# Bias tables of every second neighbourhood head in the two conditioning tiles, with the conditioning rows kept in DRAM meanwhile

## The chip, the cores and the metric

The kernel runs on one core of one Trainium2 chip. The metric is the device time of one execution in microseconds (us); less is better. A core has five engines, each with an instruction queue of its own that is worked off in order: PE (TensorE, matrix products), DVE (VectorE), ACT (ScalarE), POOL (GpSimd) and SP (SyncE, which here only issues DMA transfers). Work of different engines runs side by side unless a semaphore makes one wait for the other.

## The reference

Two layers of a diffusion backbone over 512 latent tokens and 256 context tokens, model width 1024. Both token streams are shifted, scaled and gated by vectors that come from two conditioning rows (`c` for the latent tokens, `c_ctx` for the context tokens):

```python
silu_c = jax.nn.silu(c)[:, None, :]
silu_cc = jax.nn.silu(c_ctx)[None, None, :]
for l in range(DEPTH):
    sh_a, sc_a, g_a, sh_f, sc_f, g_f = jnp.split(silu_c @ mod_w[l] + mod_b[l], 6, axis=-1)
    csh_a, csc_a, cg_a, csh_f, csc_f, cg_f = jnp.split(silu_cc @ mod_w[l] + mod_b[l], 6, axis=-1)
    a_lat, a_ctx = modulate(h_lat, sh_a, sc_a), modulate(h_ctx, csh_a, csc_a)
    ...
```

Layer 0 has 8 latent-attention heads (MLA) and 8 two-dimensional neighbourhood heads; layer 1 has sliding-window attention (SWA) with 16 heads. Each layer ends in a SwiGLU. In a neighbourhood head every query sees a patch of keys, and a learned table by relative place is added to the scores:

```python
s_lat = jnp.einsum('bnqhd,bknmhd->bhnqkm', qr, k_blk).astype(jnp.float32) * scale
s_lat = s_lat + col_bias[:, dr_idx].transpose(0, 2, 3, 1, 4)[None]
s_lat = jnp.where(col_ok[:, :, None, :], s_lat, NEG_INF).reshape(b, h, n_cb, NA_CB, kr * NA_KB)
s_ctx = jnp.einsum('bnqhd,bchd->bhnqc', qr, kc).astype(jnp.float32) * scale
p = jax.nn.softmax(jnp.concatenate([s_ctx, s_lat], axis=-1), axis=-1).astype(v.dtype)
```

## The kernel before

The program is one pass in stages, told here by the profiled execution: the start with norm, first modulation and the values of the neighbourhood heads (0 to 75 us), the input projections with modulation vectors beside them (75 to 195), the neighbourhood heads (195 to about 275), the MLA heads (to about 390), output projection and SwiGLU of layer 0 (to about 1030), SWA (about 1040 to 1180), output projection and SwiGLU of layer 1.

**Order.** The program is written as Python generators and then put in order by a scheduler that plays the program through on a timeline of its own and writes each engine's queue. A changed dependence can therefore move instructions on every engine, also far from the edit. Afterwards each queue is fixed.

**Tiles.** `T(tag, shape)` takes the next buffer of a ring of that name; `BUFS` says how many buffers a ring has, `SIZES` how many bytes each has in a partition. Writing into a buffer waits until all readers of its former tile are done. The ring `nb` has two buffers.

**Conditioning rows.** The tile `cond` holds both rows, each spread over all 128 partitions (2 x 1024 numbers). `load_cond(v)` loads row v by a DMA and applies Silu on ACT. Before that, the same tile serves for a moment as scratch for the shift terms of the values (`raw`). The rows are read by `mod_tile`: a row of `mod_w` is multiplied by the conditioning row and summed, on DVE (L237, and L215 for the late ones), or on POOL and ACT (L254, L255) for the second row during the projections. In the neighbourhood and MLA heads no modulation vector is computed; the next reader is L215 in layer 0's SwiGLU.

**Bias tables.** `nb_tiles(h)` loads the tables of head h as two tiles of the ring `nb`: the first serves query blocks 0 and 1, the second blocks 2 and 3. Heads go in pairs. A pair has three jobs: the context queries, then blocks 0 and 1 of both heads, then blocks 2 and 3 of both heads. For each block PE makes the scores in a PSUM bank (L745, L746; ring `s` of three banks), DVE adds the table and takes the row's extreme (`take`, L542, tile `p` or `wr`), ACT does the exponentials (L538), PE transposes the weights (L479), DVE or ACT copy them (L470, L471), and PE multiplies by the values (L532). With two buffers, the second head's table for blocks 0 and 1 can be loaded only when the first head's has been read in the same job.

**DMA.** All these loads are issued by SP, in order (`dma`, L134). A load whose buffer isn't free holds back what stands behind it in SP's queue.

**MLA.** `latent_operands(h)` prepares the operands of an MLA head; the rotated part of the query (`QR`) gets into the query tiles `st` by small DMA copies, also in SP's queue. The first products that read them are L1065.

Of the kernel before, what the change touches and what calls it, by code (L numbers as in the profile page):

```python
# [32 lines left out]
CTX2 = slice(NL, NT + 2)  # L33
HT = NT // 2
TOK1, TOK2 = slice(0, HT), slice(HT, NT)
BUFS = dict(b=24, part=4, st=12, wr=3, wh=3, wl=3, p=8, ph=4, pl=4, sm=10, nb=2)
SIZES = dict(b=3080, st=3072, p=3072, nb=3072, wr=4096, wh=4096, wl=4096, ph=2048, pl=2048, sm=96)
PBUFS = dict(s=3, t=2, o=1, d=2)


# [60 lines left out]
def hybrid_kernel(ctx: ExitStack, tc, I, out):  # L101
# [3 lines left out]
    dr = ctx.enter_context(tc.tile_pool(name="dr", bufs=1, space=bass.MemoryType.DRAM))  # L105
    count = [0]

    def T(tag, shape, dt=F32):
        count[0] += 1
        if tag not in SIZES:  # L110
            return sb.tile(shape, dt, tag=tag, name=f"{tag}_{count[0]}", bufs=BUFS.get(tag, 1))
        n = int(np.prod(shape[1:]))
        t = sb.tile([P, SIZES[tag] // (2 if dt == mybir.dt.bfloat16 else 4)], dt, tag=tag, name=f"{tag}_{count[0]}",
                    bufs=BUFS[tag])[: shape[0], :n]
        if len(shape) == 3:
            t = t.rearrange("p (a b) -> p a b", a=shape[1])
        return t

    def B(dt=F32, tag="b"):
        return T(tag, [P, NT], dt)  # L120
# [12 lines left out]
    def dma(o, i):  # L133
        return nc.sync.dma_start(f(o), f(i))  # L134

    V, S, G, PE = nc.vector, nc.scalar, nc.gpsimd, nc.tensor

    def f(ap):
        return ap.bitcast(F32) if ap.dtype == F32R else ap

    def const(name, shape, dt=F32):
        t = T(name if dt is F32 else "nb", shape, F32)
        dma(t, I[name])
        if dt is F32:
            return t
        r = T(name + "_r", shape, dt)
        S.copy(r, t)
        return r
# [2 lines left out]
    cond_col, pick = T("cond_col", [P, KT, 32]), T("pick", [P, 2])  # L151
    dma(cond_col, I["cond_col"])
    dma(pick, I["pick"])
    cond = T("cond", [P, 2, D])
    X = [B() for _ in range(KT)]
    for k in range(KT):
        dma(X[k][:, LATS], I["xc"][k, :, LATS])
    modb = const("modb", [P, 96])
    ident_r = const("ident", [P, P], F32R)

    def load_cond(v):
        dma(cond[:, v, :], I["cond"][v].partition_broadcast(P))
        S.activation(cond[:, v, :], cond[:, v, :], AF.Silu)

    ident = f(ident_r)
    eps = T("eps", [P, 1])
# [38 lines left out]
    def mod_tile(l, comp, m, vecs):  # L205

        at, ts, one = l * 48 + comp * 8 + m, {}, float(comp in (1, 4))
        if late:
            w = late[0]()
            dma(w, I["mod_w"][at])  # L210
            for v in vecs:
                if (l, comp, v) not in MOD:
                    MOD[l, comp, v] = T(f"mod{l}{comp}{v}", [P, 8])
                    first[l, comp, v] = m
                V.tensor_tensor_reduce(out=T("p", [P, D], mybir.dt.bfloat16), in0=w, in1=cond[:, v, :], op0=ALU.mult, op1=ALU.add,  # L215
                                       scale=1.0, scalar=0.0, accum_out=MOD[l, comp, v][:, m : m + 1])
                if m == KT - 1:
                    a = first.get((l, comp, v), 0)
                    t = MOD[l, comp, v][:, a:]
                    V.scalar_tensor_tensor(t, t, one, modb[:, at + a - m : at + 1], op0=ALU.add, op1=ALU.add)  # L220
                    for k in range(a, KT):
                        MOD[l, comp, v, k] = MOD[l, comp, v][:, k : k + 1]
            yield
            return
        for v in vecs:
            if m == 0:
                MOD[l, comp, v] = T(f"mod{l}{comp}{v}", [P, 8])
            ts[v] = MOD[l, comp, v][:, m : m + 1]
            first[l, comp, v] = m + 1
        if dense[0]:  # L230
            rs, ws = [], []
            for i in range(2):
                w, c = T(("ph", "pl")[i], [P, 512]), slice(512 * i, 512 * i + 512)
                dma(w, I["mod_w"][at, :, c])
                if 0 in vecs:
                    junk = T("p", [P, 512], mybir.dt.bfloat16)
                    V.tensor_tensor_reduce(out=junk, in0=w, in1=cond[:, 0, c], op0=ALU.mult, op1=ALU.add, scale=1.0,  # L237
                                           scalar=ts[0] if i else 0.0, accum_out=ts[0])
                ws.append(w)
            if 0 in vecs:  # L240
                V.scalar_tensor_tensor(ts[0], ts[0], one, modb[:, at : at + 1], op0=ALU.add, op1=ALU.add)
                MOD[l, comp, 0, m] = ts[0]
                yield
            if 1 in vecs:
                tile[0] += 1
                by_dve = TURN1[tile[0] % len(TURN1)] if tile[0] < MANY else 0
                for i, w in enumerate(ws):
                    c = slice(512 * i, 512 * i + 512)
                    if by_dve:
                        V.tensor_tensor_reduce(out=T("p", [P, 512], mybir.dt.bfloat16), in0=w, in1=cond[:, 1, c], op0=ALU.mult,  # L250
                                               op1=ALU.add, scale=1.0, scalar=ts[1] if i else 0.0, accum_out=ts[1])
                        continue
                    rs.append(T("part", [P, 1]))
                    G.tensor_tensor(w, w, cond[:, 1, c], op=ALU.mult)  # L254
                    S.activation(w, w, AF.Identity, accum_out=rs[i])  # L255
                if rs:
                    V.tensor_tensor(ts[1], rs[0], rs[1], op=ALU.add)
                V.scalar_tensor_tensor(ts[1], ts[1], one, modb[:, at : at + 1], op0=ALU.add, op1=ALU.add)
                MOD[l, comp, 1, m] = ts[1]
                yield  # L260
            return
        w = T("wr", [P, D])
        dma(w, I["mod_w"][at])
        for v, t in ts.items():
            junk = T("pl", [P, D], mybir.dt.bfloat16)
            V.tensor_tensor_reduce(out=junk, in0=w, in1=cond[:, v, :], op0=ALU.mult, op1=ALU.add, scale=1.0, scalar=0.0,
                                   accum_out=t)
# [598 lines left out]
    bias = PM()  # L866
    for k in range(KT):
        PE.matmul(bias[32 * (k % 4) : 32 * (k % 4) + 32], shift[:, k], raws[k], start=k < 4, stop=k > 3)
    raw = cond[:, :, :NX]
    S.copy(raw, bias.rearrange("p (v c) -> p v c", v=2))  # L870
    part = [T(x, [P, 512], F32R) for x in ("wh", "wl")]
    hi, lo = (x.rearrange("p (v c) -> p v c", v=2) for x in part)
# [7 lines left out]
    for v in range(2):  # L880
        load_cond(v)
# [7 lines left out]


    def nb_tiles(h):
        ts = [T("nb", [P, NT]) for i in range(2)]
        for i in range(2):
            dma(ts[i], I["nb"][h, i])
        cut = (slice(0, 512), slice(256, 768), slice(256, 768), slice(0, 512))
        return lambda n: ts[n // 2][:, cut[n]]
# [205 lines left out]
    i = 0  # L1102
# [44 lines left out]
    drain()  # L1147
    dense[0] = True
    late.append(lambda: T("rope0", [P, D]))


    H = []
# [576 lines left out]
    norm, ops, sums, _ = combined(H, 1, 3, *HALVES)  # L1729
# [175 lines left out]
```

## Time and profile before

| | |
|---|---|
| runs of the kernel | 1587.41 us median of 3 (1586.18 to 1589.96) |
| profiled execution | 1591.88 us, of which the span from first to last instruction is 1589.8 us |
| mean granted TensorE clock | 0.992 |
| busy share of the span | PE 97%, weight loads 86%, DVE 74%, ACT 51%, POOL 14% |
| DMA | 214.93 MB moved, mean 135 GB/s |

The profile is of one execution. Rows of the timeline give the start, the duration, the engine, the line, the operation with output and inputs, and in brackets how long the engine had been idle before it and which instruction ended that. "SPq" is the issue of a DMA on SP; its duration isn't that of the transfer. DVE instructions named CUSTOM_DVE_ANT_0 are the multiply-and-sum or add-and-take operations; the order lists below call them ISA.

### The profile page before, as it was taken

What the parts mean: (1) busy time and instruction counts of PE and PEld (TensorE: products, weight loads), DVE (VectorE), ACT (ScalarE), POOL (GpSimd) and SP (SyncE); (2) the same over time, 40 slices, a digit from 0 to 9 for tenths busy, and PEclk for the clock granted to TensorE, in tenths of its full rate; (3) what the DMA queues carried; (4) which work ended last, traced back from release to release, by engine and by line L of the source; (5) the groups of instructions that cost most, each with busy time, mean ns of one, the idle gap of its engine ahead of it and who ended that gap; (6) DMA issues with size and microseconds to landing.
All of it is one profiled execution on the core that took longest, in us unless ns stands there. A gap on an engine that the chain in (4) does not pass through costs nothing.

```text
span 1589.8 us, 26694 instructions
## 1 busy us (share of the span) xinstructions
PE 1536.5 (97%) x10034; PEld 1373.0 (86%) x10034; DVE 1182.3 (74%) x2365; ACT 806.8 (51%) x1643; POOL 225.8 (14%) x218
## 2 busy tenths in 40 slices
PE   6998989999999999999999999999999999999998
PEld 4686877787898989899999999878889998898997
DVE  4495968668589778785877776868877778687686
ACT  4364487677366324242333345557756545354463
POOL 0151724230010000000001010393002000000000
PEclk9999999999999999999999999999999999999999
DMA  9445343101562564746556555131006133233232
GB/s 342 148 162 192 102 125 101 36 11 64 180 208 86 163 233 154 240 144 214 199 191 243 194 208 207 41 104 43 2 14 198 40 108 128 87 100 114 90 103 87
DMA packets 80465, 214.93 MB, mean 135 GB/s; under 512 B 10192, under 2 KB 17872, under 8 KB 80336
## 3 DMA queue, kind: packets, MB, share of 16 engines
q1 hardware_dynamic: 73552, 188.05, 36.3%
q0 software_dynamic: 4480, 22.02, 3.6%
q10 hardware_dynamic: 2304, 3.15, 0.5%
q8 instruction: 79, 1.29, 0.3%
q14 instruction: 50, 0.41, 0.1%
HBM read 186.97 MB, written 23.07 MB: 132 GB/s over the span
## 4 chain that ended last, share of the span: by engine, by line
PE 76%; DVE 10%; DMA 7%; issue 3%; ACT 2%; POOL 2%; SPq 0%; DVEq 0%; ACTq 0%; POOLq 0%
PE pso L532 5%; PE pss L320 4%; PE pss L321 3%; PE pss L322 3%; PE pss L1343 3%; PE pss L1342 3%; PE pss L1341 3%; PE psd L320 3%; PE psd L321 3%; PE psd L322 3%; PE psd L1341 3%; PE psd L1343 3%; PE psd L1342 3%; PE pst L1343 3%; PE pst L1341 3%
## 5 line engine op out<-in xcount | busy, mean ns | idle before, releaser
L307 ACT CAST wh<-wr 128x512 fp32r<-128x512 f32 (+2 forms) x142 | 108.3, 777 | 196.3 <-DMA wr<-in_w_dn_dram 35.7
L308 DVE TENSOR_TENSOR wl<-wr,wh 128x1024 fp32r<-128x1024 f32 (+2 forms) x139 | 128.4, 931 | 75.4 <-ACT wh L307 74.8
L538 ACT ACTIVATE p<-p,sm 128x512 f32<-128x512 f32 (+3 forms) x144 | 105.1, 730 | 27.5 <-DVE sm L542 24.8
L215 DVE CUSTOM_DVE_ANT_0 p<-rope,cond 128x1024 bf16<-128x1024 f32 x64 | 77.5, 1222 | 29.8 <-DMA rope<-in_mod_w_dram 26.2
L321 PE MATMUL psd<-b,wh 128*128 128x256 f32 (+4 forms) x257 | 88.2, 343 | 0.0
L1343 PE MATMUL pss<-b,wl 128*128 128x256 f32 (+1 forms) x258 | 80.2, 311 | 4.2 <-DVE wl L1329 4.2
L1521 POOL DMA_DIRECT2D home<-p x40 | 21.6, 540 | 437.5 <-DVE p L1166 434.9
L1342 PE MATMUL pss<-b,wh 128*128 128x256 f32 (+1 forms) x258 | 80.0, 310 | 0.0
L320 PE MATMUL psd<-b,wh 128*128 128x512 f32 (+4 forms) x217 | 78.4, 361 | 1.4 <-ACT b L430 0.7
L1341 PE MATMUL pss<-b,wh 128*128 128x256 f32 (+1 forms) x258 | 79.6, 309 | 0.0
L320 PE MATMUL pss<-st,wh 128*128 128x256 f32 (+2 forms) x231 | 78.0, 338 | 0.4 <-ACT wh L307 0.4
L532 PE MATMUL pso<-ph,b 128*64 128x256 f32 (+1 forms) x384 | 78.1, 362 | 0.3 <-DVE ph L470 0.2
L532 PE MATMUL pso<-pl,b 128*64 128x256 f32 (+1 forms) x384 | 77.6, 362 | 0.7 <-DVE pl L470 0.7
L322 PE MATMUL pss<-st,wl 128*128 128x512 f32 (+2 forms) x231 | 77.8, 337 | 0.0
L322 PE MATMUL psd<-b,wl 128*128 128x512 f32 (+4 forms) x217 | 76.5, 353 | 0.0
L1343 PE MATMUL pst<-b,wl 128*128 128x384 f32 (+1 forms) x240 | 74.4, 311 | 0.3 <-DVE wl L1329 0.3
L1342 PE MATMUL pst<-b,wh 128*128 128x384 f32 (+1 forms) x240 | 74.4, 310 | 0.0
L1341 PE MATMUL pst<-b,wh 128*128 128x384 f32 (+1 forms) x240 | 74.4, 310 | 0.0
L321 PE MATMUL pss<-b,wh 128*128 128x256 f32 (+4 forms) x227 | 74.2, 328 | 0.1
L1342 PE MATMUL psd<-b,wh 128*128 128x384 f32 (+1 forms) x222 | 69.8, 314 | 0.0
L1341 PE MATMUL psd<-b,wh 128*128 128x384 f32 (+1 forms) x222 | 69.6, 314 | 0.0
L1343 PE MATMUL psd<-b,wl 128*128 128x384 f32 (+1 forms) x222 | 69.6, 314 | 0.0
(624 smaller groups left out, 5349.6 us busy)
## 6 DMA issues: line engine op xcount, KB each, us to landing
wr<-in_w_gu_dram SPq DMA_DIRECT2D x88, 512.0 KB, 4.2
rope<-in_mod_w_dram SPq DMA_DIRECT2D x48, 512.0 KB, 3.7
wr<-in_w_out_dram SPq DMA_DIRECT2D x32, 512.0 KB, 3.6
wr<-in_w_dn_dram SPq DMA_DIRECT2D x64, 256.0 KB, 2.8
p<-home SPq DMA_DIRECT2D x40, 384.0 KB, 3.9
home<-p POOLq DMA_DIRECT2D x40, 384.0 KB, 5.0
wr<-in_w_in_dram SPq DMA_DIRECT2D x21, 512.0 KB, 4.1
st<-in_mod_wp_dram SPq DMA_DIRECT2D x32, 256.0 KB, 4.7
```

Of the source, the lines that this page charges most:

```text
L215: V.tensor_tensor_reduce(out=T("p", [P, D], mybir.dt.bfloat16), in0=w, in1=cond[:, v, :], op0=ALU.mult, op1=ALU.add, scale=1.0, scalar=0.0 ...
L307: S.copy(h, r)
L308: (G if eng else V).tensor_tensor(lo, r, f(h), op=ALU.subtract)
L320: PE.matmul(o, wh[:, k], mh[:, c], start=first and k == 0, stop=False)
L321: PE.matmul(o, wh[:, k], ml[:, c], start=False, stop=False)
L322: PE.matmul(o, wl[:, k], mh[:, c], start=False, stop=last and k == n - 1)
L532: ins = PE.matmul(o[64 * i : 64 * i + 64, c], v(kt), t, start=n == 0, stop=n == len(moving[i]) - 1)
L538: S.activation(p[:, c], p[:, c], AF.Exp, bias=nm, scale=-1.0, accum_out=dn)
L1341: PE.matmul(o, wh, xh, start=first and k == 0, stop=False, skip_group_check=not first)
L1342: PE.matmul(o, wh, xl, start=False, stop=False, skip_group_check=not first)
L1343: PE.matmul(o, wl, xh, start=False, stop=k == 3, skip_group_check=not first)
L1521: G.dma_start(home[m], t)
```

## The change

The one tile `cond` becomes a list of two tiles of a new ring `cv` with two buffers of the same total size. After its Silu each row is also written to DRAM (`kept`, one partition's copy of 4 KB). `nb_tiles` takes the two tiles of an odd head from `cv` and those of an even head from `nb`, so that a pair's four tables have four buffers. After the MLA heads both rows are loaded from `kept` into new `cv` tiles, spread over the partitions again.

```diff
-BUFS = dict(b=24, part=4, st=12, wr=3, wh=3, wl=3, p=8, ph=4, pl=4, sm=10, nb=2)
+BUFS = dict(b=24, part=4, st=12, wr=3, wh=3, wl=3, p=8, ph=4, pl=4, sm=10, nb=2, cv=2)
...
-    cond = T("cond", [P, 2, D])
+    cond = [T("cv", [P, D]) for _ in range(2)]
...
+    kept = dr.tile([2, D], F32, tag="kept", name="kept")
+
     def load_cond(v):
-        dma(cond[:, v, :], I["cond"][v].partition_broadcast(P))
-        S.activation(cond[:, v, :], cond[:, v, :], AF.Silu)
+        dma(cond[v], I["cond"][v].partition_broadcast(P))
+        S.activation(cond[v], cond[v], AF.Silu)
+        dma(kept[v : v + 1], cond[v][:1])
...
-    raw = cond[:, :, :NX]
+    raw = cond[0][:, : 2 * NX].rearrange("p (v c) -> p v c", v=2)
...
     def nb_tiles(h):
-        ts = [T("nb", [P, NT]) for i in range(2)]
+        ts = [T(("nb", "cv")[h % 2], [P, NT]) for i in range(2)]
         for i in range(2):
             dma(ts[i], I["nb"][h, i])
...
     attend(mla_jobs())
     drain()
     dense[0] = True
     late.append(lambda: T("rope0", [P, D]))
+    cond[:] = [T("cv", [P, D]) for _ in range(2)]
+    for v in range(2):
+        dma(cond[v], kept[v].partition_broadcast(P))
```

The other edits only write `cond[v]` for `cond[:, v, :]`. Six lines are added ahead of the heads, so that a line of the kernel before from `mod_tile` on is found three lines later after the change (L542 is L545).

**What moves.** The order of PE is the same up to the neighbourhood heads; it differs in them, in the first MLA heads and again in SWA, and nowhere else. On ACT, at the end of the start stage: `wh` are weight casts, L471 (L474 after) copies the values of the neighbourhood heads out of the PSUM banks `pss`, `pst`, `psd`, and L163 (L165) is the Silu of a conditioning row. Before:

```order
L310 ACTIVATE wh_914<-wr_912 128x1024
L471 COPY b_700<-pss_156 128x128
L471 COPY b_700<-psd_159 128x128
L471 COPY b_701<-pss_155 128x128
L471 COPY b_702<-pss_157 128x128
L471 COPY b_701<-pst_158 128x128
L471 COPY b_702<-psd_160 128x128
L805 COPY sm_775<-pst_750 128x2
L432 ACTIVATE st_704<-pst_750,sm_775 64x256
L471 COPY b_703<-pss_156 128x128
L163 ACT_TABLE_LOAD
L163 ACTIVATE cond_67<-cond_67 128x1024
```

After:

```order
L313 ACTIVATE wh_918<-wr_916 128x1024
L474 COPY b_704<-pss_158 128x128
L474 COPY b_704<-psd_161 128x128
L165 ACT_TABLE_LOAD
L165 ACTIVATE cv_68<-cv_68 128x1024
L474 COPY b_705<-pss_157 128x128
L474 COPY b_706<-pss_159 128x128
L474 COPY b_705<-pst_160 128x128
L474 COPY b_706<-psd_162 128x128
L808 COPY sm_779<-pst_754 128x2
L435 ACTIVATE st_708<-pst_754,sm_779 64x256
L474 COPY b_707<-pss_158 128x128
```

The table load and the Silu of the row that didn't serve as scratch (`cv_68`) now stand ahead of five of the copies. On SP that row's load moved too, from behind eight `mod_w` pieces and a bias table to behind the fifth piece.

On DVE, the first pair of neighbourhood heads (`nb_1951`, `nb_1952` and after the change `nb_1955`, `nb_1956` are head 0's tables; `nb_1955`, `nb_1956` and after the change `cv_1959`, `cv_1960` head 1's; `ISA sm` reads out the extreme). Before:

```order
L542 ISA p_2026,sm_1950<-pss_2019,nb_1951 128x512
L542 ISA sm_1950 128x1
L470 COPY pl_2010<-pst_2005 128x512
L470 COPY pl_2067<-pst_2062 128x512
L542 ISA wr_2038,sm_1950<-pss_2033,nb_1955 128x512
L542 ISA sm_1950 128x1
L542 ISA p_2049,sm_1950<-pss_2042,nb_1955 128x512
```

After:

```order
L545 ISA p_2030,sm_1954<-pss_2023,nb_1955 128x512
L545 ISA sm_1954 128x1
L545 ISA wr_2042,sm_1954<-pss_2037,cv_1959 128x512
L545 ISA sm_1954 128x1
L545 ISA p_2053,sm_1954<-pss_2046,cv_1959 128x512
L545 ISA sm_1954 128x1
L473 COPY pl_2014<-pst_2009 128x512
```

Head 1's takes now stand directly behind head 0's, ahead of the copies of transposed weights.

On SP, the end of the neighbourhood heads (`st_2717<-b_2711` and `st_2718<-b_2712` are the high and low part of the first MLA head's query; after the change `st_2721<-b_2715` and `st_2722<-b_2716`). Before:

```order
L134 DMA nb_2763<-in_nb_dram 128x768
L134 DMA st_2717<-b_2711 32x768
L134 DMA nb_2764<-in_nb_dram 128x768
L134 DMA st_2718<-b_2712 32x768
L134 DMA st_3046<-b_2711 32x768
L134 DMA st_3047<-b_2712 32x768
L134 DMA st_3164<-b_2711 32x768
L134 DMA nb_9953<-in_w_dn_dram 128x384 x2
```

After:

```order
L134 DMA nb_2764<-in_nb_dram 128x768
L134 DMA cv_2768<-in_nb_dram 128x768
L134 DMA nb_9961<-in_w_dn_dram 128x384 x2
L134 DMA cv_4351<-kept 128x1024
L134 DMA st_2721<-b_2715 32x768
L134 DMA st_2722<-b_2716 32x768
L134 DMA st_3050<-b_2715 32x768
L134 DMA st_3051<-b_2716 32x768
```

The first row's reload, which waits for head 7's first table (`cv_2767`) to be read, now stands ahead of both query parts; the reload of the second follows behind the next `w_dn` pieces.

More of the change, by code (lines that the diff above doesn't have):

```diff
@@ L35 @@
 TOK1, TOK2 = slice(0, HT), slice(HT, NT)
-BUFS = dict(b=24, part=4, st=12, wr=3, wh=3, wl=3, p=8, ph=4, pl=4, sm=10, nb=2)
-SIZES = dict(b=3080, st=3072, p=3072, nb=3072, wr=4096, wh=4096, wl=4096, ph=2048, pl=2048, sm=96)
+BUFS = dict(b=24, part=4, st=12, wr=3, wh=3, wl=3, p=8, ph=4, pl=4, sm=10, nb=2, cv=2)
+SIZES = dict(cv=4096, b=3080, st=3072, p=3072, nb=3072, wr=4096, wh=4096, wl=4096, ph=2048, pl=2048, sm=96)
 PBUFS = dict(s=3, t=2, o=1, d=2)
@@ L214, in mod_tile @@
                     first[l, comp, v] = m
-                V.tensor_tensor_reduce(out=T("p", [P, D], mybir.dt.bfloat16), in0=w, in1=cond[:, v, :], op0=ALU.mult, op1=ALU.add,
+                V.tensor_tensor_reduce(out=T("p", [P, D], mybir.dt.bfloat16), in0=w, in1=cond[v], op0=ALU.mult, op1=ALU.add,
                                        scale=1.0, scalar=0.0, accum_out=MOD[l, comp, v][:, m : m + 1])
@@ L236, in mod_tile @@
                     junk = T("p", [P, 512], mybir.dt.bfloat16)
-                    V.tensor_tensor_reduce(out=junk, in0=w, in1=cond[:, 0, c], op0=ALU.mult, op1=ALU.add, scale=1.0,
+                    V.tensor_tensor_reduce(out=junk, in0=w, in1=cond[0][:, c], op0=ALU.mult, op1=ALU.add, scale=1.0,
                                            scalar=ts[0] if i else 0.0, accum_out=ts[0])
@@ L249, in mod_tile @@
                     if by_dve:
-                        V.tensor_tensor_reduce(out=T("p", [P, 512], mybir.dt.bfloat16), in0=w, in1=cond[:, 1, c], op0=ALU.mult,
+                        V.tensor_tensor_reduce(out=T("p", [P, 512], mybir.dt.bfloat16), in0=w, in1=cond[1][:, c], op0=ALU.mult,
                                                op1=ALU.add, scale=1.0, scalar=ts[1] if i else 0.0, accum_out=ts[1])
@@ L253, in mod_tile @@
                     rs.append(T("part", [P, 1]))
-                    G.tensor_tensor(w, w, cond[:, 1, c], op=ALU.mult)
+                    G.tensor_tensor(w, w, cond[1][:, c], op=ALU.mult)
                     S.activation(w, w, AF.Identity, accum_out=rs[i])
@@ L265, in mod_tile @@
             junk = T("pl", [P, D], mybir.dt.bfloat16)
-            V.tensor_tensor_reduce(out=junk, in0=w, in1=cond[:, v, :], op0=ALU.mult, op1=ALU.add, scale=1.0, scalar=0.0,
+            V.tensor_tensor_reduce(out=junk, in0=w, in1=cond[v], op0=ALU.mult, op1=ALU.add, scale=1.0, scalar=0.0,
                                    accum_out=t)
```

## The prediction

> **What bounds the kernel now.** I read the busy shares first, then the stage of the neighbourhood heads by windows, then DVE's waits there, the chain of waits, and the timeline around each idle stretch of PE.
>
> ```profile
> PE 1536.5 (97%) x10034; PEld 1373.0 (86%) x10034; DVE 1182.3 (74%) x2365; ACT 806.8 (51%) x1643; POOL 225.8 (14%) x218
> 195.00:250.00 55.00, 48.05 (x369) 37.83 (x369) 42.66 (x102) 45.02 (x104) 20.55 (x14) 1.00 0.39 113
> 205.00:210.00 5.00, 3.93 (x26) 2.65 (x22) 2.49 (x8) 4.39 (x10) 2.28 (x2) 1.00 0.46 108
> 210.00:215.00 5.00, 3.33 (x28) 2.56 (x30) 4.26 (x12) 4.41 (x12) 1.33 (x1) 1.00 0.53 170
> 225.00:230.00 5.00, 3.56 (x25) 2.83 (x24) 3.39 (x9) 4.06 (x11) 0.00 (x0) 1.00 0.75 260
> 230.00:235.00 5.00, 4.39 (x30) 3.23 (x30) 4.40 (x12) 5.00 (x13) 1.87 (x1) 1.00 0.25 82
> 245.00:250.00 5.00, 3.95 (x26) 2.67 (x23) 4.96 (x9) 2.77 (x7) 3.96 (x2) 1.00 0.07 12
> 250.00:360.00 110.00, 110.00 (x829) 89.95 (x829) 76.57 (x220) 81.43 (x188) 33.55 (x23) 1.00 0.16 45
> ```
>
> After the length of a window come PE, weight loads, DVE, ACT and POOL busy. PE is the bound nearly everywhere, so a gain can only come from PE's idle time. Between 195 and 250 us that is 55 - 48.05 = 6.95 us; from 250 to 360 there is none, so time won before 250 is kept. The whole gain that four table buffers can bring by filling idle time is therefore 7 us. How much of it hangs on the tables is told by DVE's waits and the chain:
>
> ```profile
> DVE wr L542 <- DMA nb<-in_nb_dram: 4.9, 4, 3.3
> 202.00 2.93 DMA nb<-in_nb_dram
> ...
> 224.55 4.37 DMA nb<-in_nb_dram
> 210.74 0.69 DVE L542 CUSTOM_DVE_ANT_0 wr<-pss,nb 128x512 f32<-128x512 f32 x1 [3.25 <-DMA nb<-in_nb_dram]
> 211.50 0.39 PE L745 MATMUL pss<-st,st 128*128 128x256 f32 x1 [2.35 <-DVE sm L542]
> 205.81 0.47 PE L745 MATMUL pss<-st,st 128*128 128x512 f32 x1 [0.20 <-DVE sm L542]
> 227.63 1.02 DVE L939 SCALAR_TENSOR_TENSOR b<-b,mla_gain,b 128x768 f32<-128x768 f32 x1 [0.79 <-ACT b L936]
> 229.06 0.69 DVE L542 CUSTOM_DVE_ANT_0 wr<-pss,nb 128x512 f32<-128x512 f32 x1 [0.41 <-DMA nb<-in_nb_dram]
> 229.81 0.39 PE L745 MATMUL pss<-b,b 128*128 128x256 f32 x1 [1.32 <-DVE sm L542]
> 245.00 2.27 DVE L1052 CAST st<-b 32x768 fp32r<-32x768 f32 x1
> 248.05 0.50 PE L745 MATMUL pss<-b,b 128*128 128x512 f32 x1 [1.05 <-DVE sm L542]
> ```
>
> The chain runs four times through a table load (the first and the last are shown): the second head's table is asked for only when the first head's has been read, and lands 2.9 to 4.4 us later. `wr` marks the second head's first take. While DVE waits for its table, the three score banks are full, and PE waits for a bank. That sequence stands whole at 210.74 and 211.50.
>
> **The change, part by part.**
>
> *Tables of the odd heads (gain).* Four buffers hold a pair's tables, so each can be loaded while the pair before is worked on. Where PE idles now:
>
> - First pair: 2.35 + 0.20 = 2.55 us of idle hang on `wr` takes. Not all can go: in 205 to 215 ACT is busy 4.39 + 4.41 = 8.80 of 10 us, so the stretch shrinks by 1.2 us before ACT is full. Bounds 1.2 and 2.55; neither row is nearer, so I take the middle, 1.9.
> - Second pair: 1.32 us, of which DVE's table wait is 0.41; the rest is L939, which waited 0.79 us for ACT, standing ahead of the take. In the new order the take stands ahead of L939. ACT is full from 230 on (5.00 of 5). Bounds 0.41 and 1.32; 0.9.
> - Third pair: 1.05 us behind a 2.27 us cast on DVE that stood ahead of the `wr` take. In the new order both of the head's takes precede that cast. ACT has room (2.77 of 5). Bounds 0 and 1.05; near the upper, 0.9.
> - The other 2 us of idle, and the fourth pair, where PE doesn't idle: 0.
>
> Sum 3.7 us.
>
> *The table loads themselves.* Odd-head loads must wait for the last readers of the conditioning rows. For head 1 these are the POOL and DVE products; the loads stand around the last `mod_w` pieces on SP:
>
> ```profile
> 188.89 1.28 POOL L254 TENSOR_TENSOR pl<-pl,cond 128x512 f32<-128x512 f32 x1
> 190.96 0.33 SPq L134 DMA_DIRECT2D pl<-in_mod_wp_dram  x1
> 85.99 0.33 SPq L134 DMA_DIRECT2D ph<-in_mod_w_dram  x1
> ```
>
> The last reader ends at 190.17, and the piece behind the load was issued at 190.96 anyway: 0. Both tables are then there ahead of the first pair's takes near 202. Two 4 KB stores wait on SP for the Silus, which end at 83.7 (below), while SP's next piece left at 85.99: 0.
>
> *Earlier Silu (start stage).* The row that isn't scratch is now loaded behind the fifth `mod_w` piece, and its Silu stands on ACT ahead of five copies out of PSUM. PE waits for the last of those.
>
> ```profile
> 70.97 0.38 SPq L134 DMA_DIRECT2D pl<-in_mod_w_dram  x1
> GB/s 0 0 0 0 0 0 0 90 229 373 332 295 266 274 209 250 336 393 389 395 365 387 361 381 197 262 344 410 410 426 451 410 418 410 418 426 246 98 8 0
> DMA to landing us min/median/max: 6.6/7.0/7.5
> 76.49 0.66 ACT L471 COPY b<-pss 128x128 f32<-128x128 f32 x2
> 79.36 0.16 ACT L805 COPY sm<-pst 128x2 f32<-128x2 f32 x1 [1.36 <-PE pst L322]
> 80.19 1.28 ACT L163 ACT_TABLE_LOAD   x1
> 81.48 1.06 ACT L163 ACTIVATE cond<-cond 128x1024 f32<-128x1024 f32 x1
> 82.59 1.06 ACT L163 ACTIVATE cond<-cond 128x1024 f32<-128x1024 f32 x1
> 80.22 0.51 PE L320 MATMUL pss<-b,wh 128*128 128x512 f32 x1 [0.90 <-ACT b L471]
> 82.57 0.69 DVE L237 CUSTOM_DVE_ANT_0 p<-ph,cond 128x512 bf16<-128x512 f32 x1 [1.51 <-ACT cond L163]
> 122.08 0.39 PE L320 MATMUL pst<-b,wh 128*128 128x258 f32 x1 [1.62 <-DVE st L716]
> 120.00:140.00 20.00, 16.30 (x118) 11.89 (x117) 10.88 (x19) 12.45 (x26) 0.00 (x0) 1.00 0.46 157
> ```
>
> The load takes the place at 70.97. In the GB/s row (half-microsecond slices from 66 us) 1.9 MB have moved by 76.0, and ahead of and with this row are 5 x 256 + 512 KB = 1.84 MB, so it lands near 76. ACT: 76.49 + 1.28 + 1.06 = 78.83, then four copies of together 1.1 us to 79.9, against 79.36 before: the idle 1.36 us hides most, and PE starts 0.5 us later. If the row needs the measured 7.0 us it lands at 78.4, and PE is 1.1 us later. Against that, the second Silu needs no table load and can start near 80.9 instead of 81.48, so the DVE and POOL products, on which PE's 3.70 idle us of 120 to 140 partly depend, start up to 0.5 earlier. Bounds -0.5 and +1.1; I take +0.2. [...]
>
> *Reloads.* The first reader of a reloaded row is L215 at 513.7; the reloads are free to issue from about 270 on:
>
> ```profile
> L215 DVE CUSTOM_DVE_ANT_0 p<-rope,cond x64: 1210/1224/1227, 513.7 to 908.8; 128x1024 bf16<-128x1024 f32 x64
> 268.28 0.69 DVE L542 CUSTOM_DVE_ANT_0 p<-pss,nb 128x512 f32<-128x512 f32 x1
> 269.98 0.53 SPq L134 DMA_DIRECT2D st<-b  x1
> 274.87 0.28 PE L1065 MATMUL pss<-st,st 96*128 96x256 f32 x1
> ```
>
> Their data cost nothing, with 240 us to spare. Their place on SP can: the first MLA query parts now stand behind the first reload. That waits for head 7's table, read at 268.97; SP then issues the parts near 270, as before, but they land behind 512 KB, at the 400 GB/s seen above 1.3 us later. They were issued 4.9 us ahead of L1065: 0. Upper bound, if the spread load takes its 7.0 us: 268.97 + 7.0 = 276.0, 1.1 us late.
>
> *New order in SWA.*
>
> ```profile
> 1080.00:1170.00 90.00, 89.61 (x738) 73.41 (x737) 77.57 (x279) 70.82 (x178) 8.31 (x7) 1.00 0.01 1
> PE pss L745 <- DVE sm L542: 1.7, 2, 1.2
> ```
>
> PE idles 0.39 us in 90, so the new order can win nothing and may lose; I take 0 and carry the loss as a rival.
>
> Sum: -3.7 + 0.2 = -3.5 us. The profiled execution took 1591.88 us (span 1589.8), so it would take 1588.4; it is 4.5 us above the median of the runs, 1587.41, which goes to **1583.9 us**. 0.2% (3.2 us) is about what a measurement of this kernel can tell from no change.
>
> **Rivals.**
>
> 1. *The tables are not the limit.* With them in place the next to be late is ACT, 45.02 of 55 us busy and full at 230. Then only the lower bounds come: 1.2 + 0.4 + 0 - 0.2 = 1.4, 1586.0 us. For it: ACT; where PE is full (250 to 360), ACT is only 74% busy. Against it: PE's three waits all end on a take.
> 2. *Query parts late.* The reload's 1.1 us plus at most 1 for the low part: 1583.9 + 2.1 = 1586.0. Against it: 4.9 us of margin.
> 3. *More than the idle time.* Weight loads take 89.95/110 = 0.818 of the full stretch, but 0.688 of 195 to 250. Packed as densely, the 37.83 us of loads need 46.3, a gain of 8.7 less 0.2: 1578.9. [...] The trace allows it, but ACT's 45.02 us speak against it.
> 4. *Slower, by SWA's new order.* The same wait as in the heads, PE for a bank that a take must free, lasts up to 1.2 us there. One such per pair is 8 x 1.2 = 9.6 us: 1593.5. It decides from three waits on (3.6 us). Against it: DVE has 12 us of slack in 90, and the scheduler moved only whole score groups by some ten rows.
>
> **How the numbers follow.** Forecast 0.43 (own range 1580.4, all idle gone, to 1584.2), rival 3 0.05: both faster, 0.48. Rivals 1 and 2, 0.33 and 0.05: within 0.2%, 0.38. Rival 4, 0.14: slower. The range reaches from rival 3, 1579, through 1 and 2 to rival 4 with five or six waits, 1590.5, which leaves some 0.1 above.
>
> **What would show it.** DVE's waits for tables vanish; PE's idle time from 195 to 250 falls from 6.95 to about 3.3, with the PE waits of 2.35 and 1.05 gone; PE's wait of 0.90 at 80.2 becomes about 1.4; the first MLA product comes some 3.3 us earlier, without a wait; SWA's idle stays under 1 us. I am wrong if ACT's exponentials end PE's waits in the heads, if the Silu waits for its row, or if SWA gains takes that PE waits for.

## The result, and the profile after

| | runs | median, us | against before, 95% interval |
|---|---|---|---|
| before | 16 | 1588.16 (1584.42 to 1593.55) | |
| after | 16 | 1596.01 (1591.18 to 1605.11) | 1.0050 (1.0034 to 1.0066) |

The change makes the kernel 0.5% slower; 1583.9 us was forecast, with 1590.5 as the upper end. The profiled execution of after took 1594.62 us, with a span of 1592.8. First the busy line of its page, then its windows (length, PE, weight loads, DVE, ACT and POOL busy, granted clock, DMA share, GB/s):

```profile
PE 1538.6 (97%) x10034; PEld 1373.6 (86%) x10034; DVE 1186.4 (74%) x2365; ACT 806.6 (51%) x1643; POOL 226.3 (14%) x218
195.00:250.00 55.00, 46.32 (x326) 36.67 (x327) 43.58 (x96) 42.84 (x101) 18.62 (x13) 0.89 0.39 114
205.00:215.00 10.00, 8.81 (x77) 7.53 (x76) 9.94 (x21) 8.41 (x25) 6.75 (x4) 1.00 0.53 141
225.00:230.00 5.00, 2.16 (x15) 1.96 (x16) 2.13 (x2) 4.61 (x12) 2.29 (x1) 0.80 0.16 60
230.00:235.00 5.00, 5.00 (x19) 2.44 (x18) 3.12 (x5) 3.77 (x9) 0.55 (x2) 0.52 0.18 52
245.00:250.00 5.00, 4.32 (x20) 2.91 (x22) 4.94 (x8) 2.26 (x5) 1.83 (x1) 0.50 0.27 82
250.00:360.00 110.00, 110.00 (x821) 89.16 (x818) 75.71 (x213) 78.22 (x182) 32.33 (x23) 0.99 0.15 44
1080.00:1170.00 90.00, 89.62 (x733) 73.32 (x730) 74.79 (x273) 69.52 (x174) 11.91 (x10) 0.99 0.02 8
```

Two things went wrong in the heads. PE's idle time there rose from 6.95 to 55 - 46.32 = 8.68 us, and the granted clock, 1.00 before, fell to 0.89. The sliding-window stage is as before. DVE has no wait for a table left, but PE has two new waits of over 2.5 us. After's timeline, PE, ACT, DVE and POOL rows around them (start, duration, instruction, idle time before it and what ended that):

```profile
208.05 0.39 PE L748 MATMUL pss<-st,st 128*128 128x256 f32 x1 [1.19 <-DVE sm L545]
221.65 0.28 PE L748 MATMUL pss<-b,b 128*128 128x256 f32 x1
224.66 0.83 ACT L939 COPY b<-psd 128x512 f32<-128x512 f32 x2
225.27 0.87 PE L452 MATMUL psd<-ident_r,sm 128*128 128x128 f32 x6 [0.86 <-ACT b L939]
225.39 0.73 ACT L541 ACTIVATE p<-p,sm 128x512 f32<-128x512 f32 x1
226.11 0.50 ACT L541 ACTIVATE p<-p,sm 128x256 f32<-128x256 f32 x1
226.60 1.03 ACT L310 CAST wh<-wr 128x1024 fp32r<-128x1024 f32 x1
227.53 0.51 ACT L541 ACTIVATE p<-p,sm 128x256 f32<-128x256 f32 x1
228.04 0.82 ACT L347 CAST b<-b 128x768 fp32r<-128x768 f32 x1
228.76 0.85 ACT L939 COPY b<-psd 128x512 f32<-128x512 f32 x2
229.39 1.11 PE L482 MATMUL psd<-ident_r,p 128*128 128x128 f32 x4 [2.57 <-ACT b L939]
242.09 2.38 POOL L311 TENSOR_TENSOR wl<-wr,wh 128x1024 fp32r<-128x1024 f32 x1 [3.98 <-ACT wh L310]
242.28 2.62 DVE L1055 CAST st<-b 32x768 fp32r<-32x768 f32 x1
244.92 0.69 DVE L545 CUSTOM_DVE_ANT_0 wr<-pss,cv 128x512 f32<-128x512 f32 x1
245.68 0.79 PE L748 MATMUL pss<-b,b 128*128 128x512 f32 x1 [2.56 <-DVE sm L545]
```

`latent_norms` prepares the MLA heads' inputs beside the neighbourhood heads: it calls `gained`, in which PE spreads each token's norm factor over all 128 partitions (a "spread", L452) for DVE to multiply by. At 225.27 PE writes the second spread into the two `psd` banks. ACT runs three exponentials and two casts before it copies those banks out at 228.76. A few scores later the next instruction in PE's queue is a transpose that needs a `psd` bank: 2.57 us. At 242.28 a cast stands on DVE ahead of a `wr` take, and takes 2.62 us: PE waits 2.56. Before had the same copies nearly as far apart, and the same cast (PE, ACT, DVE and POOL rows of before):

```profile
226.74 0.86 ACT L936 COPY b<-psd 128x512 f32<-128x512 f32 x2
228.00 0.37 PE L745 MATMUL pss<-b,b 128*128 128x256 f32 x1
230.51 0.84 ACT L936 COPY b<-psd 128x512 f32<-128x512 f32 x2
243.70 0.55 DVE L1052 CAST st<-b 32x768 fp32r<-32x768 f32 x1
244.46 2.40 POOL L308 TENSOR_TENSOR wl<-wr,wh 128x1024 fp32r<-128x1024 f32 x1 [3.68 <-ACT wh L307]
```

There PE's first scores of the third pair (`b,b`) came at 228.00, between the copies, and covered them. After's queue has them ahead of both spreads, at 221.65: the cover was spent. And the first cast took 0.55 us in before, where POOL began its split only at 244.46; the second one, begun within it, took 2.27.

What the clock did at each wait shows in windows cut at it, after first, then before around its longest wait:

```profile
226.60:229.40 2.80, 0.23 (x3) 0.03 (x2) 0.51 (x1) 2.80 (x8) 1.69 (x1) 0.75 0.00 0
229.40:234.60 5.20, 5.20 (x17) 2.64 (x18) 3.72 (x5) 3.58 (x8) 0.75 (x2) 0.50 0.17 50
234.60:239.00 4.40, 3.71 (x30) 3.36 (x31) 3.28 (x7) 2.96 (x8) 3.39 (x5) 0.98 0.33 119
243.10:245.70 2.60, 0.04 (x2) 0.02 (x1) 2.57 (x4) 0.85 (x4) 1.38 (x1) 0.87 0.23 91
245.70:251.70 6.00, 6.00 (x26) 3.64 (x27) 4.49 (x7) 3.32 (x8) 1.83 (x1) 0.50 0.23 68
```

```profile
209.10:211.50 2.40, 0.04 (x1) 0.00 (x1) 0.76 (x3) 2.27 (x6) 2.15 (x2) 1.00 0.75 202
211.50:216.00 4.50, 4.33 (x36) 3.11 (x37) 4.50 (x14) 4.03 (x10) 0.00 (x0) 1.00 0.43 127
```

After the wait PE looks busy, yet for 5.2 and 6.0 us it works at half the clock: 2.6 + 3.0 = 5.6 us more lost. With the 1.7 us of idle time that makes 7.3 us; from the first score of the neighbourhood heads to the first MLA product after takes 86.6 us (194.77 to 281.41), before 77.7 (197.18 to 274.87). Those two stretches, before first:

```profile
197.18:274.87 77.69, 70.74 (x540) 57.74 (x539) 60.44 (x153) 63.35 (x150) 26.16 (x20) 1.00 0.37 108
194.77:281.41 86.64, 77.96 (x561) 62.22 (x561) 66.59 (x155) 64.71 (x154) 29.28 (x22) 0.92 0.36 104
```

The 1.6 us that are left go with 21 more PE instructions in after's stretch. The two profiled executions differ by 3.0 us of span only, since after's reached the heads 2.4 us earlier and took 3.5 us less behind them. So one pair of profiles shows where the heads lose, and not how much a run loses.

Each run lists its span and mean granted clock, so its time can be split into full-clock work and waiting (span x clock) and the rest, lost to the half clock. Half clock within a wait counts as lost too, though PE loses nothing there. The table has means over 143 listed runs of before and all those of the others; three runs above 1650 us are left out. Before's own five batches lie between 1576.4 and 1577.5 us of work and 8.7 and 10.1 of half clock. The ratio is each kernel's against the runs of before beside it; idle time and heads are of the one profiled execution. The window of the idle time is fixed, while the heads begin between 193.1 and 200.1 us; and e1, whose PE order is before's, idles 5.33 us for 6.95, so a difference of 1.6 us in that column can be chance.

| kernel | median, us | ratio, 95% | span x clock | lost to clock | PE idle, 195 to 250 | first score to first MLA product |
|---|---|---|---|---|---|---|
| before | 1588.16 | | 1576.9 | 9.4 | 6.95 | 77.7 |
| after | 1596.01 | 1.0050 (1.0034-1.0066) | 1580.2 | 14.6 | 8.68 | 86.6 |
| e1 split, park | 1589.15 | 0.9998 (0.9976-1.0020) | 1576.0 | 11.9 | 5.33 | 77.3 |
| e2 first pair | 1597.38 | 1.0054 (1.0036-1.0071) | 1581.5 | 14.9 | 9.01 | 84.3 |
| e3 old order | 1589.56 | 1.0006 (0.9990-1.0022) | 1576.7 | 11.1 | 3.70 | 78.5 |
| e4 later pairs | 1588.43 | 1.0000 (0.9984-1.0017) | 1576.0 | 10.8 | 5.67 | 77.7 |
| f1 no Sqrt | 1593.69 | 1.0040 (1.0021-1.0059) | 1577.8 | 13.8 | 7.27 | 82.6 |
| f2 before, no Sqrt | 1586.53 | 1.0000 (0.9981-1.0020) | 1576.7 | 8.3 | 6.57 | 78.7 |
| f3 casts on POOL | 1592.82 | 1.0025 (1.0003-1.0046) | 1577.1 | 13.0 | 6.29 | 79.6 |
| f4 both | 1588.08 | 1.0001 (0.9982-1.0020) | 1575.0 | 10.7 | 5.17 | 77.9 |
| g1 spreads by DVE | 1593.35 | 1.0032 (1.0016-1.0049) | 1579.0 | 12.5 | 6.11 | 79.9 |
| g2 g1 and POOL casts | 1590.28 | 1.0014 (1.0002-1.0026) | 1578.5 | 9.9 | 5.61 | 79.1 |
| g3 before with g2's moves | 1588.24 | 0.9999 (0.9987-1.0010) | 1576.1 | 9.8 | 6.06 | 79.7 |
| g4 old order, POOL casts | 1584.86 | 0.9968 (0.9953-0.9983) | 1573.4 | 9.6 | 2.56 | 73.4 |
| h1 before, POOL casts | 1586.91 | 0.9990 (0.9976-1.0005) | 1575.4 | 9.4 | 4.05 | 77.9 |
| h2 g4 with two buffers | 1589.92 | 1.0009 (0.9993-1.0024) | 1578.2 | 10.1 | 5.05 | 77.7 |
| h3 g4, spreads by DVE | 1589.88 | 1.0003 (0.9988-1.0018) | 1574.6 | 12.6 | 2.68 | 75.4 |
| k1 g4, wide sums | 1582.11 | 0.9958 (0.9942-0.9975) | 1572.6 | 8.4 | 3.08 | 71.9 |
| k2 g4, sums apart | 1584.26 | 0.9972 (0.9955-0.9990) | 1573.5 | 9.1 | 3.25 | 73.2 |

Of after's 8.5 us in these means, 3.3 are waiting and 5.2 half clock.

### The profile page after: what moved, and what is told of

It is laid out like the page before. It is cut to its first block, busy times and chain, and to the rows that moved or that the text cites. A ratio compares the mean times of both kernels' runs of the same rounds, so it can differ in the third digit from the quotient of the medians.

```text
span 1592.8 us, 26722 instructions
## 1 busy us (share of the span) xinstructions
PE 1538.6 (97%) x10034; PEld 1373.6 (86%) x10034; DVE 1186.4 (74%) x2365; ACT 806.6 (51%) x1643; POOL 226.3 (14%) x218
## 4 chain that ended last, share of the span: by engine, by line
PE 72%; DVE 10%; DMA 8%; issue 6%; ACT 2%; POOL 2%; SPq 0%; DVEq 0%; ACTq 0%; POOLq 0%
PE pso L535 5%; PE pss L323 3%; PE pss L324 3%; PE pss L325 3%; PE psd L323 3%; PE psd L324 3%; PE psd L325 3%; PE pss L1349 3%; PE pss L1348 3%; PE pss L1347 3%; DMA wr<-in_w_gu_dram 3%; PE pst L482 2%; PE pst L1349 2%; PE pst L1347 2%; PE pst L1348 2%
## 5 line engine op out<-in xcount | busy, mean ns | idle before, releaser
L218 DVE CUSTOM_DVE_ANT_0 p<-rope,cv 128x1024 bf16<-128x1024 f32 x64 | 77.6, 1223 | 35.4 <-DMA rope<-in_mod_w_dram 30.4
L323 PE MATMUL psd<-b,wh 128*128 128x512 f32 (+4 forms) x217 | 77.9, 359 | 4.1 <-DVE st L719 2.1
L1347 PE MATMUL pss<-b,wh 128*128 128x256 f32 (+1 forms) x258 | 79.7, 309 | 0.0
L325 PE MATMUL pss<-st,wl 128*128 128x512 f32 (+2 forms) x231 | 77.7, 337 | 0.0
```

The lines of the kernel that those rows point to most:

```text
L323: PE.matmul(o, wh[:, k], mh[:, c], start=first and k == 0, stop=False)
L325: PE.matmul(o, wl[:, k], mh[:, c], start=False, stop=last and k == n - 1)
L1347: PE.matmul(o, wh, xh, start=first and k == 0, stop=False, skip_group_check=not first)
```

## The experiments

**Which part of the change costs it (e1 to e4).** e1 keeps the rows' way through DRAM (the "park" of its text) and drops the tables; e2 gives `cv` to head 1 alone, e4 to heads 3, 5 and 7.

```
-        ts = [T(("nb", "cv")[h % 2], [P, NT]) for i in range(2)]
+e1:     ts = [T("nb", [P, NT]) for i in range(2)]
+e2:     ts = [T("cv" if h == 1 else "nb", [P, NT]) for i in range(2)]
+e4:     ts = [T("cv" if h in (3, 5, 7) else "nb", [P, NT]) for i in range(2)]
```

> The whole change except the tables: all eight heads take their tables from the two `nb` buffers again; the conditioning rows are still two tiles, parked and reloaded. PE's order is that of before from the first to the last row. Theory A (heads: the new order makes two PE waits of about 2.6 us, each of which halves the granted clock for some 3.3 us of lost work): nothing of that is left, so 1588 us, within 2.5 of before; between 195 and 250 us PE is busy about 48 us at clock 1.00 and DVE's waits for tables are back. Rival B (stores, reloads or the earlier Silu cost the time): 1594 to 1598, the loss ahead of 195 us or behind 270. Rival C (the new order in the sliding-window stage costs it): 1588 too, not told apart from A here.

> Only head 1 takes its table from `cv`; heads 3, 5 and 7 from `nb`. PE's order is that of the changed kernel up to the middle of the second pair and again from the MLA stage on, the sliding-window stage included. Theory A: the first of the two new PE waits (before a `p` transpose, for ACT's copies of line 939) stands, with its half clock: +5.9 us, less about 2 for the table waits of the first pair, so 1591 to 1593; the second wait (third pair) is not there or is a shorter one. Rival B: 1594 to 1598, as the changed kernel. Rival C: 1594 to 1598 as well, with PE idle or slow between 1040 and 1180 us.

> Heads 3, 5 and 7 take their tables from `cv`, head 1 from `nb`. PE's order in the first pair and up to the middle of the second is that of before; from the MLA stage on it is that of the changed kernel. Theory A: the first new wait is gone and PE waits 2.35 us for head 1's table at full clock again, as before; if the second new wait (third pair, for a take behind the casts of line 1055) stands, with its half clock, 1590 to 1593, otherwise 1586 to 1588. Rivals B and C: 1594 to 1598.

e3 has all the tables, but writes an odd head's loads where the bias is first used, and orders each (for the scheduler only, without a wait on the chip) behind the last take written until then, `taken[-1]`, an even head's:

```
+        def table(n):
+            if n // 2 in left:
+                left.remove(n // 2)
+                behind(dma(ts[n // 2], I["nb"][h, n // 2]), *(taken[-1:] if h % 2 else ()))
+            return ts[n // 2][:, cut[n]]
```

> All four odd heads take their tables from `cv`, but the loads are written behind the even head's takes and the scheduler is told to put them behind them, so the heads come in another order than in either kernel, nearer that of before. The sliding-window stage has the changed kernel's order. Theory A: the time goes by the PE waits in the heads alone: with no wait over 2.4 us and clock 1.00 in 195 to 270 us it is 1584 to 1588; with one wait of 2.5 us or more and its half clock 1588 to 1592. Rivals B and C: 1594 to 1598 whatever the heads show.

e1, e3 and e4 are as fast as before; e2 alone has the whole loss. Its time alone would fit rivals B and C as well; e1, e3 and e4 exclude them. So the park, the reloads and the earlier Silu cost nothing that can be measured (e1), nor does the new order of the sliding-window stage, which e2, e3 and e4 share with after. One head's tables, head 1's, are enough. e2 is 4 us slower than I expected; its profile has the second wait too, for a copy of transposed weights (`ph`) that stands on DVE behind a 2.63 us cast. e3 has no wait above 1.13 us and yet isn't the 1584 to 1588 of that case: its clock is 0.97 there (k1 and k2 come back to that). PE in e2:

```profile
229.17 0.66 PE L482 MATMUL psd<-ident_r,p 128*128 128x128 f32 x4 [2.57 <-ACT b L939]
244.44 0.69 PE L535 MATMUL pso<-ph,b 128*64 128x256 f32 x1 [2.56 <-DVE ph L473]
```

**Are these two waits the loss (f1 to f4).** f1 puts Identity for the square root in `gained`, so ACT's two table loads around it go (the kernel leaves the root out); f2 does so in before; f3 moves the casts of L1055 to POOL; f4 does both to after. In f1 only the two loads leave ACT's order, and PE's and DVE's are after's to the last row.

```
-            S.activation(col[:, c], d[:, c], AF.Sqrt, bias=eps, scale=1.0 / (P * len(tiles)))
+f1, f2, f4: S.activation(col[:, c], d[:, c], AF.Identity, bias=eps, scale=1.0 / (P * len(tiles)))
-                    V.tensor_copy(KA[s][i][ROPE[s]], KR[i][:32])
+f3, f4:             G.tensor_copy(KA[s][i][ROPE[s]], KR[i][:32])
```

> The changed kernel with Identity in place of Sqrt in `gained` (leaves that square root out), so ACT's two table loads of 1.28 us at 220.2 and 221.9 go; every engine's order is otherwise the changed kernel's. Theory A (the loss is two PE waits of 2.57 and 2.56 us in the heads with the half clock behind them): the first wait, for ACT's second copy of line 939, shrinks by about as much as ACT is relieved, 2.56 us, to about 0, its half clock goes too, the second wait stays: 1590 to 1593. Rival D (ACT as a whole, or the new order as a whole, is too slow in the heads, and the wait only moves to the next ACT instruction): 1594 to 1596, with PE's idle time of 195 to 250 us still above 8.

> The kernel before with the same replacement (leaves the square root of `gained` out). The control of the run above: in before PE does not wait for the two table loads. Theory A: 1587 to 1589, no change that can be measured. If two table loads fewer are worth 2.6 us anywhere, 1585.

> The changed kernel with the four casts of line 1055 (the rotary keys into `KA`, 32x768, up to 2.62 us each on DVE) on POOL. PE's order differs from the changed kernel's in seven short pieces of the third pair. Theory A: the second wait (2.56 us, for a take behind such a cast) goes with its half clock, the first stays: 1590 to 1593. Rival D: 1594 to 1596.

> Both edits on the changed kernel (the square root of `gained` left out, casts on POOL). Theory A: both waits gone, clock 1.00 from 195 to 250 us, PE idle there under 4.5 us: 1585 to 1588, so faster than before or the same. Rival D: 1592 to 1596.

f3 came as Theory A has it: without the second wait a quarter of a per cent is left. f4's time did (1588.08, level with before), its profile did not: 5.17 us of idle time, not under 4.5, and a clock of 0.97, not 1.00. f1 stays 0.4% slower, and its first wait is still there. The intervals of f1, f3 and after overlap, so only f4 is clear of after. PE in f1:

```profile
231.57 0.66 PE L482 MATMUL psd<-ident_r,p 128*128 128x128 f32 x4 [2.45 <-ACT b L939]
246.84 0.80 PE L748 MATMUL pss<-b,b 128*128 128x512 f32 x1 [2.55 <-DVE sm L545]
```

So the table loads are not what the first wait is made of. Both of its ends move with them; the five instructions between the spread and the copies stay between. f4 kept a 2.44 us wait there too and was level all the same, and what it gained over f3 is not explained: its profile has f3's wait, and the same loads gave before nothing (f2).

**The first wait by itself (g1 to g3).** The spreads are written ahead of the gains, and DVE copies them out:

```
+        for i in range(len(groups)):
+            rs.append(B())
+            for c in (LATS, CTXS):
...
+                with shifted(-FIRST):
+                    spread(d, [col[:, y : y + 1].to_broadcast([P, P]) for y in range(x, x + n)])
+                    V.tensor_copy(rs[i][:, c], d[:, : n * P])
```

> The changed kernel; in `gained` all four spreads are written ahead of the gains, and the copies out of PSUM (line 939 of the changed kernel) stand on DVE instead of ACT. PE's order is the changed kernel's as far as the third pair. The run without the table loads left the wait before the `p` transpose at 2.45 us, so the table loads are not what it consists of; Theory A2: it is ACT's order, in which three exponentials and two casts stand between PE's second spread and the copies that free the two `psd` banks. On DVE, idle there, the copies come within 1 us: the wait of 2.57 us falls below 0.7, its half clock goes, the second wait stays or moves: 1590 to 1593. Rival D (PE has run out of scores and the next thing it needs, the exponentials, is as late as the copies): a wait of 1.5 us or more remains there, now for ACT's line 541, and 1593 to 1596.

> The run above with the casts of line 1055 on POOL as well, nothing left out. Theory A2: both waits gone, 1584 to 1588: faster than before by up to 0.2% or the same. Rival D: 1589 to 1593.

> The kernel before with the same two moves (spreads first with their copies on DVE, casts on POOL), without the tables. The control: what the moves give alone. Theory A2: PE doesn't wait for either of them in before, except 1.05 us behind a cast in the third pair: 1585 to 1589. If it is as fast as the run above, the extra tables give nothing even when their new waits are taken away.

The wait fell as theory A2 has it (PE in g1):

```profile
231.91 0.66 PE L482 MATMUL psd<-ident_r,p 128*128 128x128 f32 x4 [0.58 <-DVE b L941]
```

The clock stayed at 1.00 from 195 to 275 us in that execution. But the time came back by a third only, 0.32% for 0.50%, with intervals that overlap, and just above what I expected; g2, with the casts moved as well, is clear of after but still 0.14% behind before, and the same moves give before nothing (g3). In g1 new waits of 1.03 and 1.12 us for DVE stand at 237.8 and 241.9; DVE is busy 49.99 us from 195 to 250, against 43.58 in after. Taking the two waits away does not bring the tables' gain in this order; Theory A2's 1584 to 1588 for g2 was wrong; 1590.28 lies in the range of rival D, by which the waits only move on.

**Is there a gain in the tables at all (g4, h1 to h3).** g4 is e3 with the casts on POOL; h1 moves the casts in before; h2 is g4 with all tables in `nb`; h3 is g4 with g1's copies.

> The kernel whose odd-head loads are written behind the even head's takes, with the casts of line 1055 on POOL. Theory A2: it had a wait of 1.1 us for a take and one of 0.9 for ACT's line 939 left; 1586 to 1589, no measurable gain over before. If the extra tables are worth their 3.7 us in some order, it shows here: 1584.

> The kernel before with the casts of line 1055 on POOL, two table buffers. Theory A3 (the 0.32% of the fast order is the extra tables', as forecast, once no new wait takes it): 1586.5 to 1588.5, at most the 1.05 us wait behind a cast gained, so no measurable change. Rival E (the moved casts give it): 1583 to 1585.

> The fast kernel (loads written behind the takes, casts on POOL, rows parked) with every table in the two `nb` buffers: all of it but the extra tables. Theory A3: DVE waits for tables again and PE's waits for `wr` takes come back, 2.3 and 1 us, PE idle 195 to 250 us about 6 to 7 instead of 2.6: 1587 to 1590. Rival E, or the loads' new place: 1583 to 1586.

> The fast kernel with the spreads of `gained` first and their copies on DVE. It has 2.56 us of PE idle time left between 195 and 250 us, of which one wait of 0.94 is for ACT's copies of line 949. Theory A3: that wait falls below 0.6 us: 1584 to 1585.5, not to be told from the fast kernel. If the copies delay takes on DVE: 1586 to 1589.

g4 is 0.32% faster than before, 5 us, where Theory A2 had no gain, and its idle time is what was forecast for after or less. PE's largest waits there, the window, and h2's wait for tables:

```profile
PE psd L482 <- ACT b L949: 0.9, 1, 0.9
PE pss L750 <- DVE sm L545: 0.9, 1, 0.9
195.00:250.00 55.00, 52.44 (x413) 44.13 (x412) 42.18 (x117) 48.29 (x119) 20.45 (x15) 0.97 0.44 136
```

```profile
DVE wr L545 <- DMA nb<-in_nb_dram: 2.2, 2, 2.0
```

The casts alone (h1) and all but the extra buffers (h2) give nothing measurable; the intervals of g4 and h2 do not meet. So the 0.3% come with the extra buffers. Whether they are the buffers' own or the order's isn't told apart: h2's order isn't g4's, since the scheduler follows the buffers. h3 missed: its full-clock work and waiting is 1574.6 us, 2.3 below before's, but the half clock takes 3 us more than in before and it is level; its profile has a new wait of 1.63 us for a DVE copy.

**The half clock without a wait (k1, k2).** In e3, g4 and h3 the clock halves near 214 to 217 us with no idle time in front (h3: 0.61 from 216 to 220 us, PE busy throughout). PE in g4: the product group ahead of it, the window of that group and the one behind:

```profile
212.20 2.06 PE L937 MATMUL psd<-ones,b 128*128 128x1 f32 x18
212.20:214.20 2.00, 2.00 (x21) 2.00 (x20) 1.71 (x6) 1.95 (x7) 0.00 (x0) 1.00 0.87 212
214.20:217.60 3.40, 3.40 (x19) 3.40 (x19) 1.17 (x3) 3.37 (x6) 0.00 (x0) 0.53 0.79 273
```

k1 makes these sums 32 columns wide; k2 puts a `yield` behind each tile's sums.

```
-                PE.matmul(d[:, i * m + j : i * m + j + 1], acc[:, j * P : (j + 1) * P], ones[:, :1], ...
+k1:             PE.matmul(d[:, 32 * (i * m + j) : 32 * (i * m + j) + 32], acc[:, j * P : (j + 1) * P], ones[:, :32], ...
```

> The fast kernel with the `ones` products of `gained` 32 columns wide instead of one, into 32 columns of the same bank; as many products. Theory F (the clock falls because a run of single-column products streams hardly anything): the dip near 214 us is gone or shorter, mean clock 0.001 to 0.002 higher than the fast kernel's 0.994, 1582 to 1584. Rival G (the dip has another cause there, or 32 columns are still too few): the dip stays behind the same products, 1584 to 1586.

> The fast kernel with a pause between the `ones` products of each tile in the program's order: the row of nine products (18 records) becomes one of seven and a piece of two later. Theory F: the dip near 214 us is rarer, 1582 to 1585, if the new order brings no other wait. Rival G: it stays, 1584 to 1586.

PE in k1, the same group and its windows:

```profile
210.60 2.09 PE L937 MATMUL psd<-ones,b 128*128 128x32 f32 x18
210.60:212.70 2.10, 2.10 (x22) 2.10 (x21) 1.71 (x6) 2.04 (x7) 0.00 (x0) 1.00 0.81 186
212.70:216.10 3.40, 3.40 (x34) 3.12 (x35) 1.95 (x5) 3.37 (x6) 0.00 (x0) 1.00 0.91 285
```

As long, as many, and the clock stays up: three of three profiles with 18 single-column records in a row dip, the one with wide products and the one with 14 in a row (k2) do not. In the other 14 profiles there are at most 10 in a row, and no half clock begins within 4 us behind any such row. (k2 has one at 233.7, behind a wait of 1.70 us.) k1 is the fastest kernel of the study, 0.42% under before (0.9958, 0.9942 to 0.9975). With one profile each and orders that differ in short pieces, Theory F is supported and not settled; k1's and g4's intervals overlap.

## Why the prediction was wrong, step by step

- *Table waits vanish, reloads free, first MLA product without a wait, sliding-window order 0*: right. After's DVE has no table wait, e1 shows the reloads and the earlier Silu together, and after's query parts leave SP from 274.20 on, 7.2 us ahead of L1068. That product was forecast 3.3 us earlier; it came 6.5 us later (281.41 for 274.87). Rival 2 falls. Rival 4's size (1593.5) was close, its place wrong: e3 and e4 carry its order and lose nothing.

```profile
77.92 1.06 ACT L165 ACTIVATE cv<-cv 128x1024 f32<-128x1024 f32 x1
80.40 0.51 PE L323 MATMUL pss<-b,wh 128*128 128x512 f32 x1 [0.96 <-ACT b L474]
274.20 0.58 SPq L134 DMA_DIRECT2D st<-b  x1
281.41 0.36 PE L1068 MATMUL pss<-st,st 96*128 96x256 f32 x1
```

- *Earlier Silu, +0.2 us*: PE's wait is 0.96 us where 0.90 stood; 1.4 was forecast. The first Silu did not hold the copies back as feared.
- *First pair, 1.9 us*: 2.55 us of waiting became 1.19 (208.05 above), 1.36 gained, inside the bounds, but that may be luck. The 2.35 us was one execution's: in seven profiles with two buffers for the first pair this wait is 2.35 to 2.53 three times (before, e4, f2) and 1.13 to 1.25 four times (e1, g3, h1, h2), as in after. What fills up is not ACT (8.41 of 10 us) but DVE, 9.94 of 10 in 205 to 215.
- *Second pair, 0.9 us*: **the step that failed.** The 1.32 us wait went, but 0.86 and 2.57 us for ACT's copies came. (By its tiles that wait was already in the third pair: only its queries and keys have the tag `b`.) I had read that ACT was full from 230 us on and drew from it only that a gain would be small. In the order made for four buffers the third pair's scores stand earlier on PE, and those were what covered ACT's long order between the copies. I priced a gain as time taken off, and left out that work done earlier is missing as cover later. Rival 1 (ACT next) named the engine, but with a floor of 1.4 us gained: it had no way to lose.
- *Third pair, 0.9 us*: 1.05 us became 2.56. "In the new order both of the head's takes precede that cast" holds for the second of the two casts; the first still stands ahead of them, and now runs beside POOL's split, at 2.62 us for 0.55.
- *A term that was not there*: the half clock, +5.2 us of the loss in the means. Before's row read 1.00 and I took it as a property of the stage. It was one execution: f2, with before's order, has 0.97 there after a 2.53 us wait:

```profile
208.27 0.38 PE L745 MATMUL pss<-st,st 128*128 128x256 f32 x1 [2.53 <-DVE sm L542]
```

- *The size of the tables' gain*: 3.7 us is about what one order gives: h2 to g4 is 4.3 us in the heads (77.7 to 73.4, one profile each) and 0.4% between the two ratios. The parts it was summed from did not come so. The change as made does not get it.

That the order (e3 against after, with the same buffers) decides is shown. That the two waits and their half clock are most of the loss is read from the profiles and supported by g2; how the loss divides between them isn't shown. Why the scheduler chose after's order is not shown either, and which of the many differences between g2's and g4's orders is worth their 0.46% stays open.

## What to carry to other kernels

A wait removed early on can mean that an in-order engine uses up the work that covered a later stall (in after PE's scores of the third pair, at 221.65 for 228.00, and then a wait of 2.57 us): for each gain, ask what the engine will do with the time, and what then stands unhidden. Where a scheduler orders the program, a buffer more is a new order; try several orders of the same change before it is judged, since here the same four table buffers gave +0.50% (after), +0.06% (e3) and, with the casts moved too, -0.32% (g4). A wait of PE had to be priced here with the clock that followed it: 0.50 for 5.2 and 6.0 us behind after's waits of 2.57 and 2.56 us.

## What the runs showed of the hardware

A DVE cast (L1052, L1055; 32x768, SBUF to SBUF) that began while POOL ran a two-input TENSOR_TENSOR ended only 0.41 to 0.45 us after POOL's instruction did: all twelve such single casts in nine profiles, at 0.55 to 2.66 us each; all six with POOL idle at their start took 0.55. Two casts that run into one another took 1.02 us together in before, from 253.30, with POOL idle until 254.31; beside a TENSOR_TENSOR and two MEMSETs of POOL such a pair took 2.69 us in e2, 3.00 in g1 and 4.01 in e3. No run varied POOL alone, and what held the casts isn't shown.

The granted clock halved behind waits of PE for which I had allowed nothing. The clock records of before's and after's traces have 1.00 and 0.50 and nothing between. Over the 19 profiles, of the PE waits between 192 and 282 us that lasted 2.35 to 2.57 us, 10 of 11 were followed by (or ended in) a clock of 0.50; of the 28 of 1.0 to 1.8 us, 4 were. At after's two waits of 2.57 and 2.56 us the half clock lasted 6.83 us each time (from 227.98 and from 245.04). In e1, behind a wait of 1.23 us, it lasted 3.4 us:

```profile
209.88 0.38 PE L748 MATMUL pss<-st,st 128*128 128x256 f32 x1 [1.23 <-DVE sm L545]
211.10:214.50 3.40, 3.40 (x22) 2.57 (x22) 3.40 (x10) 3.35 (x10) 0.00 (x0) 0.50 0.62 168
```

Behind g4's row of 18 single-column products, 2.06 us of a PE that the profile calls busy, the clock was 0.53 over 3.4 us; behind k1's row of 18 products 32 columns wide, 2.09 us, it was 1.00. What decides whether the clock halves isn't shown.
